# Softmax denominators inverted over 8 columns instead of 512, with the values moved by DMA, in an attention block inside a two-layer encoder trunk

## The chip, the cores and the metric

One Trainium2 chip; the kernel runs on one of its cores. The metric is the device time of one execution in microseconds (us). The engines of a core go by the profile's short names: PE is TensorE (matmuls, and PEld its weight loads), DVE is VectorE, ACT is ScalarE, POOL is GpSimd, SP is SyncE, whose queue issues nearly all DMAs here. Each engine works through its own queue strictly in the order in which the program was written; engines wait for one another by semaphores. SBUF is the on-chip memory of 128 partitions, PSUM the matmul results' memory of eight banks.

## The reference

Two layers, each on x of 512 tokens x 1024 channels in float32:

```python
h = rms_norm(x, attn_norm_g[l])
proj = h @ w_in[l]          # MLA latents, GQA q/k/v, pool channels, 3 branch gates
o_mla  = mla_branch(...)    # 8 heads, q and k of 96 (64 + 32 rotary), v of 64
o_gqa  = gqa_branch(...)    # 8 heads, 2 kv heads, 64 wide, rotary
o_pool = pool_branch(...)   # centred mean pooling
merged = sum(gate_i * (o_i @ w_branch_i))
x = x + merged @ w_out[l]
x = x + (silu(u_gate) * u_val) @ ffn_w_down[l]   # u: conv of width 3 over rms_norm(x) @ ffn_w_up
```

In both attention branches every head is, over all 512 tokens,

```python
p = softmax(q @ k.T * scale)     # 512 x 512
o = p @ v                        # 512 x 64
```

What matters here is the softmax's division: o = (exp(s - m) @ v) / (sum of exp(s - m)), one divisor for each head and token.

## The kernel before

**Precision and matmuls.** Every operand of a matmul is split into a rounded part and a remainder (names ending in h and l, such as wh and wl, ph and pl, oh and ol). A product is three matmuls of the parts. ACT makes the rounded part by a copy, and DVE or POOL makes the remainder by a subtraction. Weights stream in: SP loads pieces of 512 KB into three buffers (raw), ACT makes wh, DVE or POOL makes wl.

**Order.** No scheduler reorders anything: the order on every engine is the order in which the Python code emits instructions. That order is decided by a small planner, class Clock. It keeps an estimated time, an event heap, and for every engine the time at which it would be free. A chain of steps (`chain`) runs one step after the other: each step emits its instructions when the planner's time reaches the end of the step before it. `ck.fin` is that end; a step can set it by hand. `pick` and `copy` choose the engine for a subtraction or a copy by which one the planner holds to be free first (POOL or DVE, and ACT or DVE).

**Attention.** `attention(kind, fill, okey, odst)` runs once for GQA and once for MLA in each layer. Heads 0 to 7 overlap: a table `plan` places each head's steps in time, and between them `fill` emits matmuls of another kind (the gates, the branch projection of the branch finished last, and during GQA the making of MLA's q, k and v with their norms). So PE always has filler work in its queue between the dependent steps of attention. For one head:

- `t_q` (and `t_k` for MLA): transposes q (and k) to channels x tokens, tiles qa, qb, kh, kl;
- `s_max`: scores of 128 queries x 512 keys into the one PSUM bank ps_S, and on DVE their negated row maximum, nm (L224), four times;
- `m_row`: a small matmul turns the four maxima into rows, and DVE writes them into qb (GQA) or qa (MLA), from where a matmul subtracts them;
- `probs`: scores with keys on the partitions, four times 128 keys x 512 queries, into ps_ST; ACT takes the exponential (pe), then ph and pl are made;
- `av_hi`, `av_lo`: values x probabilities into ps_AV. The stationary operand holds a head's 64 value columns and 64 columns of ones, so partitions 0 to 63 of ps_AV are the output and partitions 64 to 127 all hold the same row of 512 sums;
- `o_out(h)`: two heads share the tiles oraw and osum (an even head in partitions 0 to 63, an odd one in 64 to 127). ACT copies the 64 rows of sums and the 64 rows of output out of PSUM. After the odd head DVE inverts osum, 128 x 512, in four reciprocals of 128 columns (L236), multiplies oraw by it, and oh (ACT) and ol (POOL; DVE for the last pair) are made for the branch projection.

The reciprocal works on all 128 partitions, of which 64 and 64 hold the same row. Four pairs a call, four calls: 16 pairs, 64 reciprocals. The branch projection that reads oh and ol of GQA is filler of the MLA attention, and that of MLA comes after the MLA attention.

Of the kernel before, what the change touches and what calls it, by code (L numbers as in the profile page):

```python
# [10 lines left out]
F32 = mybir.dt.float32  # L11
F32R = mybir.dt.float32r
I32 = mybir.dt.int32
AF = mybir.ActivationFunctionType
ALU = mybir.AluOpType
# [3 lines left out]
P = 128  # L19
T = 512  # L20
# [97 lines left out]
class Clock:  # L118
# [37 lines left out]
    def done(self, *key):  # L156
        self.ready[key] = self.fin + self.SEM
# [10 lines left out]
    def chain(self, *steps, after=0.2):  # L168

        def go(n, source=None):  # L170
            if n == len(steps):
                return
            keys, fn = steps[n] if isinstance(steps[n], tuple) else ((), steps[n])
            late = [self.ready.get(k, self.now + 0.5) for k in keys]
            if late and max(late) > self.now:
                self.at(max(late) - self.now, lambda: go(n))
                return
            self.fin, self.source, self.last = self.now, source, None
            fn()
            source, self.source = self.last, None  # L180
            self.at(max(0.0, self.fin - self.now), lambda: go(n + 1, source))
        self.at(after, lambda: go(0))
# [61 lines left out]
def trunk(ctx: ExitStack, tc: tile.TileContext, x, w, prm, gb, cst, out):  # L244
    nc = tc.nc
    ctx.enter_context(tc.manual_schedule())
    ck = Clock()
    at, need, done, chain = ck.at, ck.need, ck.done, ck.chain
    V, A, G = Engine(ck, nc.vector, "DVE"), Engine(ck, nc.scalar, "ACT"), Engine(ck, nc.gpsimd, "Pool")
    PE, SY = nc.tensor, nc.sync  # L250
# [7 lines left out]
    dp = ctx.enter_context(tc.tile_pool(name="dp", bufs=1, space=bass.MemoryType.DRAM))  # L258

    uid = [0]  # L260

    def slot(name, dt=F32):
        uid[0] += 1
        t = sp.tile([P, SLOT], dt, tag="s", name=f"{name}_{uid[0]}")
        return t

    def small(name, shape, dt=F32, bufs=2):
        uid[0] += 1
        t = sm.tile(shape, dt, tag=name, name=f"{name}_{uid[0]}", bufs=bufs)
        return t  # L270
# [12 lines left out]
    def free(tag):  # L283
        heapq.heappush(banks[tag], ck.fin + ck.SEM)
# [86 lines left out]
    def split(hi, lo, src, scale=None, eng=None):  # L371

        steps = []
        if scale is None:
            steps.append(lambda: A.activation(hi, src, AF.Copy))
            steps.append(lambda: (eng or V).tensor_tensor(lo, src, f(hi), ALU.subtract))
        else:
            steps.append(lambda: A.activation(hi, src, AF.Copy, scale=scale))
            steps.append(lambda: V.scalar_tensor_tensor(lo, src, scale, f(hi), ALU.mult, ALU.subtract))
        return steps  # L380
# [108 lines left out]
    def layer(l, sq, xsrc):  # L489
# [510 lines left out]
        def attention(kind, fill, okey, odst):  # L1000
# [156 lines left out]
            def av_lo(h, k):  # L1157
                s = hs[h]
                need(key("pl", h, k))
                vh, vl = vals(h, k)  # L1160
                pl = s.pop(("p", k))[1]
                mm(s["av"], vh, pl[:, :T], False, k == 3)
                if k == 3:
                    o_out(h)

            def o_out(h):
                s = hs.pop(h)
                if h % 2 == 0:
                    ot[:] = [slot("oraw"), slot("osum")]
                raw, sums = ot  # L1170
                js = slice(64 * (h % 2), 64 * (h % 2) + 64)

                def copies():
                    A.activation(sums[js, :T], s["av"][64:128], AF.Copy)
                    A.activation(raw[js, :T], s["av"][0:64], AF.Copy)
                    free("AV")

                def recip(b):
                    bs = slice(b * P, b * P + P)
                    V.reciprocal(sums[:, bs], sums[:, bs])  # L1180

                steps = [copies]
                if h % 2 == 1:
                    oh, ol = slot("oh", F32R), slot("ol", F32R)
                    odst[h // 2] = (oh, ol)
                    steps += [lambda b=b: recip(b) for b in range(4)]
                    steps += [lambda: V.tensor_tensor(raw[:, :T], raw[:, :T], sums[:, :T], ALU.mult),
                              *split(oh[:, :T], ol[:, :T], raw[:, :T], eng=V if h == 7 else G),
                              lambda: done(okey, l, h // 2)]
                chain(*steps)  # L1190
# [67 lines left out]
        for m in range(KC):  # L1258
            tag = tags[m % 3]
# [54 lines left out]
        for c in range(FC):  # L1314
            for part in range(2):
                tag = tags[n % 3]
# [12 lines left out]
        for m in range(KC):  # L1329
            tag = tags[m % 3]  # L1330
# [14 lines left out]
            steps = [resid]  # L1345
# [161 lines left out]
```

## Time and profile before

| | us |
|---|---|
| median of 3 runs | 1699.12 |
| range of the 3 runs | 1698.81 to 1700.99 |
| the profiled execution, its own time | 1701.64 |
| span of the profiled execution | 1699.4 |
| GQA attention, layer 0, from the end of its first pair | 163 to 245 |
| MLA attention, layer 0 | 245 to 373 |
| the same two, layer 1 | 1003 to 1085 and 1085 to 1213 |

The span runs from the first to the last instruction. The profile is one execution, so its stages and durations add up to its own time and not to the median. Busy shares of PE come from modelled ends of matmuls. In the lines of the profile, `out<-in` names tiles without their numbers, xN counts instructions, and "nm L224" means the group of instructions that write nm from line 224. L216, L220, L224, L232 and L236 are the lines of the planner's wrappers for tensor_tensor, scalar_tensor_tensor, tensor_reduce, tensor_copy and reciprocal, so many different steps share a line and are told apart by their tiles. L209 is the same for ACT's activation, L341 for matmuls, L298 for the weight loads on SP.

### The profile page before, as it was taken

The page shows a single profiled execution, that of the slowest core. Times are in us where ns is not written, and L with a number is a line of the kernel's source. Part 1 is how long each engine was busy: PE and PEld are TensorE (multiplying, and loading weights), DVE is VectorE, ACT ScalarE, POOL GpSimd, SP SyncE. Part 2 cuts the span into 40 slices and gives each one's busy share as a digit, 9 for nine tenths or more (in the row PEclk, how much of TensorE's full clock was granted, in tenths as well). Part 3 has the DMA queues.
Part 4 walks back from the last instruction along what each step waited for, and adds up shares of the span by engine and source line. Part 5 has one row for each costly group of instructions (what it writes and reads, how often), then busy time and mean ns, then how long its engine had stood idle before and what let it go on. Part 6 is the DMA issues. An engine that isn't in the chain of part 4 may idle for free.

```text
span 1699.4 us, 20370 instructions
## 1 busy us (share of the span) xinstructions
PE 1655.1 (97%) x7360; PEld 1335.7 (79%) x7360; DVE 938.3 (55%) x1502; ACT 782.6 (46%) x1375; POOL 972.3 (57%) x771
## 2 busy tenths in 40 slices
PE   8889999999999999999999899999999999999999
PEld 7767767778888888888888677777788888888887
DVE  6765976643356666630156759766433666666100
ACT  5356655653344444433234576556534444444221
POOL 4455565764566566655545565666645665666543
PEclk9999999999999999999999999999999999999999
DMA  5221112113423332333333211111233232232331
GB/s 176 85 72 44 56 48 62 38 62 112 124 87 89 98 100 87 100 106 116 100 101 95 70 44 47 61 49 38 75 118 118 87 100 92 94 94 93 111 118 56
DMA packets 44596, 145.40 MB, mean 86 GB/s; under 512 B 5072, under 2 KB 6352, under 8 KB 44496
## 3 DMA queue, kind: packets, MB, share of 16 engines
q1 hardware_dynamic: 44352, 144.10, 27.0%
q8 instruction: 58, 0.95, 0.2%
q14 instruction: 42, 0.34, 0.1%
q10 hardware_dynamic: 144, 0.01, 0.0%
HBM read 139.90 MB, written 4.19 MB: 85 GB/s over the span
## 4 chain that ended last, share of the span: by engine, by line
PE 87%; DVE 8%; issue 2%; ACT 1%; POOL 1%; DMA 0%; SPq 0%; POOLq 0%; DVEq 0%; ACTq 0%
PE ps_acc L341 40%; PE ps_ST L341 23%; PE ps_AV L341 20%; PE ps_S L341 2%; DVE gqr L216 1%; PE ps_mi L345 1%; DVE yt L216 1%; DVE nm L224 1%; POOL wl L216 1%; PE ps_mi L341 1%; DVE MQ L216 1%; DVE yt L220 0%; DVE win L216 0%; DVE y L220 0%; DVE y L228 0%
## 5 line engine op out<-in xcount | busy, mean ns | idle before, releaser
L216 POOL TENSOR_TENSOR wl<-raw,wh 128x512 fp32r<-128x512 f32 (+1 forms) x514 | 678.5, 1330 | 493.4 <-ACT wh L209 432.1
L209 ACT ACTIVATE wh<-raw 128x512 fp32r<-128x512 f32 (+3 forms) x522 | 313.8, 608 | 194.2 <-PE ps_ST L341 70.8
L220 DVE SCALAR_TENSOR_TENSOR a<-u,prm,a 128x512 f32<-128x512 f32 x176 | 239.6, 1362 | 79.2 <-ACT a L209 74.0
L341 PE MATMUL ps_acc<-HH,wh 128*128 128x512 f32 x624 | 247.1, 396 | 2.2 <-DVE XM L220 2.2
L341 PE MATMUL ps_acc<-HH,wl 128*128 128x512 f32 x624 | 246.7, 395 | 1.2 <-POOL wl L216 1.2
L341 PE MATMUL ps_acc<-HL,wh 128*128 128x512 f32 x624 | 246.2, 395 | 0.0
L216 POOL TENSOR_TENSOR pl<-pe,ph 128x512 fp32r<-128x512 f32 x105 | 138.9, 1325 | 110.4 <-ACT ph L209 70.4
L341 PEld LDWEIGHTS ps_acc<-HH,wh 128*128 128x128 f32 x624 | 117.5, 188 | 30.8 <-ACT mns L209 2.1
L341 PEld LDWEIGHTS ps_acc<-HH,wl 128*128 128x128 f32 x624 | 117.3, 188 | 30.0 <-POOL wl L216 2.5
L341 PEld LDWEIGHTS ps_acc<-HL,wh 128*128 128x128 f32 x624 | 117.5, 188 | 26.8
L209 ACT ACTIVATE pe<-ps_ST 128x512 f32<-128x512 f32 x128 | 76.3, 596 | 101.8 <-PE ps_ST L341 100.4
L224 DVE TENSOR_REDUCE nm<-ps_S 128x1 fp32r<-128x512 f32 x128 | 87.8, 686 | 57.3 <-PE ps_S L341 57.0
L216 POOL TENSOR_TENSOR al<-a,ah 128x512 fp32r<-128x512 f32 x44 | 58.1, 1320 | 84.8 <-ACT ah L209 56.5
L341 PE MATMUL ps_AV<-HH,wh 128*128 128x512 f32 x256 | 101.3, 396 | 0.0
L341 PE MATMUL ps_AV<-HH,wl 128*128 128x512 f32 x256 | 101.2, 395 | 0.0
L341 PE MATMUL ps_AV<-HL,wh 128*128 128x512 f32 x256 | 101.1, 395 | 0.0
L341 PE MATMUL ps_ST<-HH,wh 128*128 128x512 f32 x240 | 95.0, 396 | 0.0
L341 PE MATMUL ps_ST<-HH,wl 128*128 128x512 f32 x240 | 94.8, 395 | 0.0
L341 PE MATMUL ps_ST<-HL,wh 128*128 128x512 f32 x240 | 94.8, 395 | 0.0
L209 ACT ACTIVATE a<-u,prm 128x512 f32<-128x512 f32 x88 | 71.8, 816 | 32.4 <-DVE u L216 32.4
L209 ACT ACTIVATE ah<-a 128x512 fp32r<-128x512 f32 x44 | 27.8, 632 | 116.2 <-DVE u L240 110.8
L209 ACT ACTIVATE a<-a 128x512 f32<-128x512 f32 x44 | 27.8, 633 | 113.5 <-DVE u L240 113.5
(332 smaller groups left out, 3563.3 us busy)
## 6 DMA issues: line engine op xcount, KB each, us to landing
raw<-w SPq DMA_DIRECT2D x229, 512.0 KB, 3.5
raw<-w SPq DMA_DIRECT2D x13, 384.0 KB, 3.0
XM<-x SPq DMA_DIRECT2D x16, 256.0 KB, 3.8
raw<-w SPq DMA_DIRECT2D x6, 448.0 KB, 3.4
xsp<-XM SPq DMA_DIRECT2D x8, 256.0 KB, 2.0
XM<-xsp SPq DMA_DIRECT2D x8, 256.0 KB, 3.2
out<-XM SPq DMA_DIRECT2D x8, 256.0 KB, 2.5
raw<-w SPq DMA_DIRECT2D x4, 432.0 KB, 3.2
```

The source lines that it names most:

```text
L209: return self.eng.activation(out, in_, func, **k)
L216: return self.eng.tensor_tensor(out, *a)
L220: return self.eng.scalar_tensor_tensor(out, *a)
L224: return self.eng.tensor_reduce(out, in_, *a, **k)
L341: PE.matmul(o, lhsT=lhsT, rhs=rhs, start=start, stop=stop)
L345: PE.transpose(o, src, ident)
```

## The change

It concerns only `o_out`. For the first three pairs of heads of every call the four reciprocals of 128 columns go. In their place stand a chain of five steps:

1. the copy of the sums takes one row of the 64 equal ones (partition 0 for the even head, 64 for the odd one);
2. `spread`: two DMAs on SP's queue lay each row of 512 sums out as 64 partitions x 8 columns (tile few);
3. `recip`: one reciprocal of 128 partitions x 8 columns on DVE;
4. `write`: one DMA brings the 1024 inverted values to a DRAM tile (line), as two rows of 512;
5. `read`: two DMAs read each row back with a broadcast to 64 partitions (tile oinv), and the multiplication uses oinv.

The planner is told 5, 5 and 6 us for the DMA steps by `ck.fin`, so it places what follows that much later in the order of each engine. The last pair of each call (heads 6 and 7) keeps the copy of 64 rows and the four reciprocals.

```diff
             def o_out(h):
                 s = hs.pop(h)
+                direct = h // 2 == 3
                 if h % 2 == 0:
                     ot[:] = [slot("oraw"), slot("osum")]
                 raw, sums = ot
-                js = slice(64 * (h % 2), 64 * (h % 2) + 64)
+                i = h % 2
+                js = slice(64 * i, 64 * i + 64)
 
                 def copies():
-                    A.activation(sums[js, :T], s["av"][64:128], AF.Copy)
+                    top = 64 * i + (64 if direct else 1)
+                    A.activation(sums[64 * i:top, :T], s["av"][64:64 + top - 64 * i], AF.Copy)
                     A.activation(raw[js, :T], s["av"][0:64], AF.Copy)
                     free("AV")
 
-                def recip(b):
-                    bs = slice(b * P, b * P + P)
-                    V.reciprocal(sums[:, bs], sums[:, bs])
-
                 steps = [copies]
-                if h % 2 == 1:
+                if i == 1:
                     oh, ol = slot("oh", F32R), slot("ol", F32R)
                     odst[h // 2] = (oh, ol)
-                    steps += [lambda b=b: recip(b) for b in range(4)]
-                    steps += [lambda: V.tensor_tensor(raw[:, :T], raw[:, :T], sums[:, :T], ALU.mult),
+                    inv, line = sums, None
+                    if direct:
+                        def recip(b):
+                            bs = slice(b * P, b * P + P)
+                            V.reciprocal(sums[:, bs], sums[:, bs])
+
+                        steps += [lambda b=b: recip(b) for b in range(4)]
+                    else:
+                        few, inv = small("few", [P, 8]), slot("oinv")
+                        uid[0] += 1
+                        line = dp.tile([2, T], F32, tag="line", name=f"line_{uid[0]}", bufs=4)
+
+                        def spread():
+                            for j in range(2):
+                                SY.dma_start(few[64 * j:64 * j + 64], sums[64 * j:64 * j + 1, :T])
+                            ck.fin = ck.now + 5.0
+
+                        def recip():
+                            V.reciprocal(few, few)
+
+                        def write():
+                            SY.dma_start(line.rearrange("j (p f) -> (j p) f", f=8), few)
+                            ck.fin = ck.now + 5.0
+
+                        def read():
+                            for j in range(2):
+                                SY.dma_start(inv[64 * j:64 * j + 64, :T], line[j].partition_broadcast(64))
+                            ck.fin = ck.now + 6.0
+
+                        steps += [spread, recip, write, read]
+                    steps += [lambda: V.tensor_tensor(raw[:, :T], raw[:, :T], inv[:, :T], ALU.mult),
                               *split(oh[:, :T], ol[:, :T], raw[:, :T], eng=V if h == 7 else G),
                               lambda: done(okey, l, h // 2)]
                 chain(*steps)
```

Since the planner now places the steps of these pairs elsewhere and holds DVE to be free earlier, the order of the instructions on all engines differs from the first pair's end on, in both attentions.

## The prediction

> **What bounds the kernel now.** I read the page first, then a table of stages by windows, then TensorE's waits, then VectorE's timeline in the stretch where TensorE waits. On the page:
>
> ```profile
> span 1699.4 us, 20370 instructions
> PE 1655.1 (97%) x7360; PEld 1335.7 (79%) x7360; DVE 938.3 (55%) x1502; ACT 782.6 (46%) x1375; POOL 972.3 (57%) x771
> ```
>
> TensorE (PE) is busy for 97% and the change takes no matmul away, so only the 44 us in which PE stands can be won. The windows of layer 0's attention (columns: length, then busy us of PE, weight load, DVE, ACT, POOL, granted clock, DMA):
>
> ```profile
> 163.00:190.00 27.00, 23.53 (x109) 18.49 (x107) 22.22 (x33) 20.00 (x38) 15.93 (x13) 1.00 0.12 39
> 190.00:245.00 55.00, 50.93 (x227) 38.79 (x226) 49.77 (x83) 35.97 (x64) 32.80 (x27) 0.97 0.14 45
> 245.00:373.00 128.00, 127.86 (x597) 101.78 (x596) 77.38 (x114) 71.85 (x128) 83.49 (x75) 1.00 0.17 53
> 186.60:190.00 3.40, 0.70 (x3) 0.61 (x4) 3.30 (x6) 0.00 (x0) 1.77 (x2) 1.00 0.13 31
> 190.00:193.40 3.40, 3.40 (x10) 2.63 (x9) 3.40 (x7) 1.75 (x3) 0.24 (x1) 0.50 0.30 123
> ```
>
> The GQA attention from its first pair on (first two rows) has 7.5 us of idle PE; the MLA attention (third row) has 0.1 us, so there the change can win nothing. In the last two rows PE stands 2.7 us and is then granted 0.50 of its clock for 3.4 us: matmuls start 0.43 us apart instead of 0.233, which costs 1.6 us more. Layer 1 repeats it (7.3 us idle, 2.55 us of it before 1029.66, then 0.50 until 1033.1). All that could be won is 7.5 + 7.3 + 2 x 1.6 = 18 us. PE's waits between 140 and 260 us say on whom:
>
> ```profile
> PE ps_S L341 <- DVE nm L224: 4.3, 4, 2.7
> PE ps_acc L341 <- DVE XM L220: 1.1, 2, 0.6
> PE ps_acc L341 <- DVE vml L216: 0.9, 1, 0.9
> ```
>
> VectorE (DVE): there is one bank for the scores whose row maximum is taken (ps_S), so each next score matmul waits until DVE's nm has read the last. The longest wait ends with this nm; note what stands ahead of it, and how long:
>
> ```profile
> 184.46 0.19 DVE L216 TENSOR_TENSOR yt<-y,ssm 128x32 f32<-128x32 f32 x1
> 184.68 1.18 DVE L220 SCALAR_TENSOR_TENSOR yt<-yt,y 128x32 f32<-128x32 f32 x1
> 185.90 1.30 DVE L220 SCALAR_TENSOR_TENSOR y<-yt,y 128x32 f32<-128x32 f32 x1
> 187.24 1.18 DVE L216 TENSOR_TENSOR yt<-y,ssm 128x32 f32<-128x32 f32 x1
> 188.46 0.19 DVE L220 SCALAR_TENSOR_TENSOR yt<-yt,y 128x32 f32<-128x32 f32 x1
> 188.56 0.68 DVE L224 TENSOR_REDUCE nm<-ps_S 128x1 fp32r<-128x512 f32 x1
> ```
>
> These are rsqrt steps, not reciprocals. From 181.3 to 232.9 us DVE's timeline has not one row with idle time before it: in this stretch DVE's queue sets PE's pace. Four reciprocals stand in it (pair 1, 202.9 to 210.5); pair 0's stand before it, pair 2's (233.6 to 237.0) behind it, with 2.4 us of DVE idle after them.
>
> **What is removed and added.**
>
> ```profile
> L236 DVE RECIPROCAL osum<-osum x64: 890/941/955, 165.5 to 1216.5; 128x128 f32<-128x128 f32 x64
> L216 DVE TENSOR_TENSOR oraw<-oraw,osum x16: 679/1098/1668, 173.4 to 1220.4; 128x512 f32<-128x512 f32 x16
> ```
>
> Removed: 12 of 16 pairs x 4 = 48 reciprocals x 0.94 = 45 us of DVE. Added on DVE: 12 reciprocals of 8 columns; 7.4 ns a column from this row gives 0.06, and DVE's smallest steps take 0.15 to 0.19, so 0.15 us each, 2 us. The order of the changed program shows what the planner makes of the rest: it gives DVE 22 casts to ph and 2 MK copies that ACT had, and 14 of POOL's pl subtractions: 22 x 0.43 + 2 x 0.69 + 14 x 0.69 = 21 us. Of 45 us, some 22 stay. ACT's sums copy keeps its 512 columns (0.59 us), on 1 partition instead of 64: nothing.
>
> In the MLA attention and everywhere else PE has no idle time, DVE has 40% spare: worth nothing, and it costs nothing as long as that spare time covers the new waits.
>
> **The GQA stretch, per layer.** Per pair the order puts: spread issued after the sums copy; small reciprocal some four DVE steps later; write; read; the multiplication 20 DVE steps on. In DVE's gapless stretch the sum from 181.3 is: four reciprocals away, -3.5; pair 0's multiplication now in it, +1.1; one small reciprocal, +0.15; four more casts, +1.7; an MK copy, +0.7; a reduction that slips in, +0.5. Net +0.6: DVE is no freer here. What does move is the order. The planner puts the row maxima of the last heads ahead of the end of the k norm: yt, yt, ssm, six MK and one XM, which took 6.5 us between 223.0 and 232.9, stand behind the last qb instead of ahead of it. That qb came at 232.9 and comes at 232.9 + 0.6 - 6.5 = 227.0, 5.9 us earlier. PE's matmul that feeds it stands nine 512-wide matmuls (9 x 0.233 = 2.1 us) earlier in PE's own order, which were not saved but put behind. So PE gains 3.8 us. Against that: the first nm after the rsqrt start is now early, but the second stands behind five rsqrt steps and pair 0's multiplication, and head 4's first score waits for its qa, which by the same sum ends at about 204.6, where PE, its matmuls counted in the order at 0.233 us from the first hole on, is there at 202.3. I see two holes of about 2.3 to 2.5 us. They are paid already, since DVE sets the pace, but another half clock (1.6 us) can follow one; at one in two, 0.8 us. Gain: 3.8 - 0.8 = 3.0 us per layer, 6.0 in all. From nothing (the holes cost it all) to 6.5 a layer is possible (7.5 + 1.6 = 9.1, less the waits on vml, mqs and mns that stay, 1.8, and 0.8 of holes); I take 3.0, the sum by the rows.
>
> **The transfers.** Nothing shows transfers this small. The nearest rows (KB, us from issue to landing):
>
> ```profile
> xsp<-XM SPq DMA_DIRECT2D x8, 256.0 KB, 2.0
> XM<-xsp SPq DMA_DIRECT2D x8, 256.0 KB, 3.2
> gb<-gb SPq DMA_DIRECT2D x2, 256.0 KB, 5.1
> prm<-prm SPq DMA_DIRECT2D x1, 89.0 KB, 5.3
> prm<-prm ACTq DMA_DIRECT2D x1, 11.5 KB, 2.9
> ```
>
> Spread and write: 2.0 to 5.3, taken 2.9 (the smallest transfer). Read, 256 KB broadcast in two: 3.2 to 6.4 (the longer gb), taken 4. An issue takes SP 0.33 us. Pair 1: sums copied at 201.5 as now, two issues, spread there at 205.1 (207.5 at worst), small reciprocal not before 206.8; write there at 210.2, read there at 214.9, at worst 220.3; the multiplication's turn is about 217.7. So it is covered by 2.8 us, and missed by 2.6 at worst. The Trainium skill ("DMA: Bandwidth & Descriptors", the anatomy of one DMA) states a fixed cost of about 2.0 us for each; three in turn would land the read at about 212, and the sum would stay; no run here shows it for 32-byte pieces.
>
> On SP the write waits for DVE and the read for the write, with weight loads behind both. raw issued at 183.24 is first read at 204.11 (3.4 us to land), and ACT's list of waits in the attentions has none on raw: some 17 us cover a held queue. ACT's oh and POOL's ol stand in their queues behind each multiplication; the first reader of oh and ol of these pairs comes after the GQA attention (b0, at about 256), of MLA's after the MLA attention.
>
> **Rivals.** (B) The holes eat it: every nm moved forward is paid by a qa or nm moved back. For: +0.6 us of DVE work in the stretch. Against: 6.5 us of steps provably leave its front. Gain 0 to 1.5 a layer: 1697.5, the same.
>
> (C) The landing is late, and this ends slower. Place: pair 1's multiplication in GQA, in DVE's gapless stretch, with head 5's nm behind it and PE behind them. It begins to cost once the chain from small reciprocal to landing passes 10.8 us (206.9 to 217.7), and outweighs the gain by 0.2% once it is about 3 us late (3 + 1.6 of half clock - 3.0 = 1.6 a layer). The rows' highest values make the chain 0.33 + 5.3 + 0.66 + 6.4 = 12.7; if one of the two also queues behind a 512 KB load (3.5 us on the page), 16.2, 5.4 late: 5.4 + 1.6 - 3.0 = 4.0 slower per layer, 1707.1. Against: SP issues a weight load only every 5 to 16 us here.
>
> (D) Exempt work is exchanged for exposed work. Rows: reciprocals keep to 890 to 955 ns, while DVE casts to ph run 398/427/1025 and pl 681/691/1795, long when POOL is in a TENSOR_TENSOR. If each of the 5 casts and copies added to the gapless stretch waits half of POOL's 1.3 us, 3.3 us come back on DVE, the 3.0 are gone, and the time is 1699.7. The median of 427 speaks against so many. The Trainium skill states this as an exclusive lock of a port pair that VectorE and GpSimd share ("SBUF — State Buffer", two separate sides), held by a VectorE instruction with two SBUF inputs or in a two-port mode; by that rule alone the exchange gives (D)'s 1699.7. The 1.18 and 1.30 us rows above, beside POOL's pl from 184.52 to 187.15, agree with it.
>
> That the change does nothing is excluded: the order has 48 fewer reciprocals and 60 new transfers.
>
> **Numbers.** The profiled execution took 1701.64 us (span 1699.4 and 2.2 around it); it lies 2.5 above the median of 1699.12. 1701.64 - 6.0 = 1695.6, which against the median is 1693.1. About 0.2%, 3.4 us, is what a measurement of this kernel tells from no change. Chances: forecast (A) 0.52, faster; (B) 0.18 and (D) 0.10, same; (C) 0.20, slower. The range goes from 1686 (both layers at 6.5) to 1704, which leaves out the upper half of (C) and little else; (A) alone is 1686 to 1695.7.
>
> **What would show it.** Right: PE idle in 163 to 245 falls from 7.5 to about 5 with the k norm's MK steps after the last row maximum; small reciprocals near 0.15 us; DVE total down by some 22 us; no DVE wait on a DMA in attention. (C): "DVE oraw <- DMA oinv" or "DVE few <- DMA few" among DVE's waits, in the GQA stretch. (D): long ph and pl on DVE. A hole over 2.5 us with 0.50 granted behind it in a place that has none now, or any PE idle in 245 to 373, would make the forecast wrong.

## The result, and the profile after

The changed kernel is slower: 1704.99 us, the median of 8 executions (1703.62 to 1707.51), against 1700.31 us for the kernel before on the same chip (8 executions, 1698.81 to 1703.23). The ratio is 1.0027, with a 95% interval of 1.0016 to 1.0038, so 2.7 to 6.5 us. A later comparison gave 1.0026 (1.0016 to 1.0036). The forecast was 1693.1 us.

The profiled execution took 1705.09 us, 3.45 more than that of the kernel before. Its page:

```profile
span 1703.1 us, 20481 instructions
PE 1656.8 (97%) x7360; PEld 1341.4 (79%) x7360; DVE 928.4 (55%) x1504; ACT 768.2 (45%) x1351; POOL 964.5 (57%) x757
```

DVE lost 48 reciprocals, 45 us, and its busy time fell by only 9.9 us. The windows (length, busy us of PE, weight load, DVE, ACT, POOL, granted clock, DMA):

```profile
163.00:190.00 27.00, 24.45 (x114) 19.98 (x113) 19.10 (x36) 19.15 (x37) 16.46 (x14) 0.98 0.14 45
190.00:245.00 55.00, 50.20 (x218) 38.04 (x217) 47.72 (x79) 30.57 (x55) 32.72 (x25) 0.95 0.18 55
245.00:373.00 128.00, 126.88 (x589) 100.21 (x589) 77.41 (x116) 69.67 (x123) 76.48 (x68) 1.00 0.19 60
220.60:224.00 3.40, 0.68 (x2) 0.50 (x2) 3.37 (x6) 0.08 (x1) 2.06 (x2) 0.89 0.00 0
224.00:227.40 3.40, 3.40 (x11) 2.52 (x10) 3.19 (x11) 0.00 (x0) 0.00 (x0) 0.61 0.00 0
```

In GQA (first two rows) PE idles 7.35 us, as long as before (7.5), but the granted clock is lower: 27 x 0.02 + 55 x 0.05 = 3.3 us of clock are lost where 55 x 0.03 = 1.65 were, so two stretches at half clock and not one. The last two rows show the second: PE stands 2.7 us ahead of 223.5, at a place where it did not stand long before, and is slow behind it. MLA (third row), which had 0.1 us of idle PE, has 1.1; in layer 1 it had 0.2 and has 2.5. The two long stalls of PE, and the sums of its waits between 140 and 260 us:

```profile
189.34 0.80 PE L341 MATMUL ps_S<-ka,qa 128*128 128x512 f32 x1 [2.55 <-DVE nm L224]
223.47 0.79 PE L341 MATMUL ps_S<-ka,qa 128*128 128x512 f32 x1 [2.72 <-DVE nm L224]
...
PE ps_S L341 <- DVE nm L224: 6.1, 4, 2.7
PE ps_acc L341 <- DVE vml L216: 0.9, 1, 0.9
```

The waits on XM are gone, those on the row maximum nm have grown from 4.3 to 6.1. DVE's timeline ahead of the new hole, and POOL's beside it:

```profile
217.06 0.68 DVE L216 TENSOR_TENSOR oraw<-oraw,oinv 128x512 f32<-128x512 f32 x1
217.66 1.40 DVE L216 TENSOR_TENSOR kj<-krt 128x128 f32<-128x128 f32 x1
218.98 2.54 DVE L216 TENSOR_TENSOR rp<-krt,tabm 128x64 f32<-128x64 f32 x2
221.45 1.37 DVE L216 TENSOR_TENSOR krr<-krt,tabm 128x128 f32<-128x128 f32 x1
222.73 0.68 DVE L224 TENSOR_REDUCE nm<-ps_S 128x1 fp32r<-128x512 f32 x1
...
217.11 3.10 POOL L216 TENSOR_TENSOR pl<-pe,ph 128x512 fp32r<-128x512 f32 x2
220.17 1.27 POOL L216 TENSOR_TENSOR ol<-oraw,oh 128x512 fp32r<-128x512 f32 x1
221.40 1.26 POOL L216 TENSOR_TENSOR wl<-raw,wh 128x512 fp32r<-128x512 f32 x1
```

kj, rp and krr are the square and the rotation of the keys' rotary part, for the k norm of MLA. They take 5.07 us from 217.66 to the start of nm, and POOL subtracts without a pause beside them. In the kernel before the same rows take 1.19 us from start to nm:

```profile
215.75 0.79 DVE L216 TENSOR_TENSOR kj<-krt 128x128 f32<-128x128 f32 x1
216.47 0.35 DVE L216 TENSOR_TENSOR rp<-krt,tabm 128x64 f32<-128x64 f32 x2
216.74 0.28 DVE L216 TENSOR_TENSOR krr<-krt,tabm 128x128 f32<-128x128 f32 x1
216.94 0.68 DVE L224 TENSOR_REDUCE nm<-ps_S 128x1 fp32r<-128x512 f32 x1
```

The new transfers in the list of DMAs (KB, median us from issue to landing):

```profile
few<-osum SPq DMA_DIRECT2D x24, 2.0 KB, 2.6
line<-few SPq DMA_DIRECT2D x12, 4.0 KB, 1.5
oinv<-line SPq DMA_DIRECT2D x24, 128.0 KB, 3.1
```

The small reciprocals and the products that use them (ns: shortest, median, longest; first and last start):

```profile
L236 DVE RECIPROCAL few<-few x12: 189/193/203, 171.2 to 1202.1; 128x8 f32<-128x8 f32 x12
L216 DVE TENSOR_TENSOR oraw<-oraw,oinv x12: 673/682/1787, 185.3 to 1213.2; 128x512 f32<-128x512 f32 x12
```

DVE's list of waits has two on the new transfers, both in layer 1 and both for the third pair of a call: in GQA the product waits 1.3 us for oinv, at 1093.35 us, and in MLA the small reciprocal waits 2.2 us for few, at 1202.15. Behind the first PE does not wait: its last stall in that stage ends at 1087.9 us.

```profile
1093.35 0.69 DVE L216 TENSOR_TENSOR oraw<-oraw,oinv 128x512 f32<-128x512 f32 x1 [1.35 <-DMA oinv<-line]
1202.15 0.20 DVE L236 RECIPROCAL few<-few 128x8 f32<-128x8 f32 x1 [2.18 <-DMA few<-osum]
```

To place the loss I measured, in every run's trace, two stages between fixed matmuls: GQA from the first transposition of GQA's second group of queries (gqr) to the first of MLA's queries (MQ), and MLA from there to the first matmul on mgh, the merged branches. Windows at half clock move a GQA stage from one execution to the next (in the changed order 112.0 to 114.7 us in layer 0, 111.3 to 113.3 in layer 1), so differences of 1 or 2 us between two profiles are not read in GQA; MLA of one order repeats within 0.7 us. A stall in the text below is the extra distance from one matmul's start to the next; the idle time that the profile prints is some 0.2 us less (the 2.55 and 2.72 above are stalls of 2.7 and 2.9). All ratios are to the kernel before on the same chip. Runs are named by their first letters.

| kernel | GQA, layers 0 and 1 | MLA, layers 0 and 1 | ratio to before, 95% interval |
|---|---|---|---|
| before | 113.1, 112.3 | 185.4, 185.2 | 1 |
| changed | 113.7, 113.0 | 187.1, 187.4 | 1.0027 (1.0016 to 1.0038) |
| e9: changed, again | 113.9, 113.1 | 187.0, 187.6 | 1.0026 (1.0016 to 1.0036) |
| e1: before, no reciprocals | 113.0, 113.8 | 185.2, 185.2 | 0.9996 (0.9985 to 1.0007) |
| e2: changed, no transfers | 112.0, 113.3 | 186.9, 187.1 | 1.0010 (1.0000 to 1.0020) |
| e13: before, with dead transfers | 114.2, 113.5 | 185.3, 185.1 | 0.9992 (0.9982 to 1.0001) |
| e3: changed, rotary steps early | 110.1, 109.6 | 186.9, 187.4 | 1.0005 (0.9995 to 1.0015) |
| e4: before, rotary steps early | 112.5, 112.3 | 185.4, 185.4 | 1.0030 (1.0016 to 1.0043) |
| e6: changed, rotary steps in the idle place | 110.5, 109.8 | 187.0, 187.5 | 0.9986 (0.9977 to 0.9995) |
| e14: before, the same place | 114.3, 115.2 | 185.3, 185.2 | 1.0008 (0.9996 to 1.0020) |
| e16: before, in its widest gap | 113.8, 113.3 | 185.4, 185.3 | 1.0004 (0.9993 to 1.0014) |
| e15: changed, POOL's pl of GQA without inputs | 108.3, 108.1 | 187.0, 187.5 | 0.9963 (0.9948 to 0.9978) |
| e5: changed, MLA's pl back | 114.0, 113.3 | 187.0, 187.5 | 1.0009 (1.0000 to 1.0018) |
| e19: changed, MLA's pl and ph back | 114.7, 113.2 | 186.4, 186.6 | 0.9999 (0.9991 to 1.0007) |
| e18: changed, POOL's pl of MLA without inputs | 114.7, 113.1 | 187.0, 187.6 | 1.0017 (1.0008 to 1.0025) |
| e8: e6 and e5 together | 110.5, 109.4 | 186.9, 187.1 | 0.9985 (0.9976 to 0.9994) |
| e10: the change in GQA alone | 113.3, 111.3 | 185.1, 185.4 | 0.9996 (0.9987 to 1.0005) |
| e11: the change in MLA alone | 114.6, 113.9 | 186.8, 187.1 | 1.0017 (1.0007 to 1.0027) |
| e12: e10 with the steps in the idle place | 110.6, 109.3 | 185.3, 185.2 | 0.9961 (0.9948 to 0.9975) |
| e17: e12 again | 110.3, 109.7 | 185.3, 185.2 | 0.9952 (0.9937 to 0.9968) |

The four stages are 5.3 us longer in the changed kernel's profile (0.7, 1.7, 0.7, 2.2). The rest of the trace, whose work is the same, is 1.6 us shorter, which is within what it varies by from run to run: the 1258 matmuls from mgh to the next stage, for one, took 291.2 to 292.7 us over all these runs, in no relation to the kernel.

### The profile page after: what moved, and what is told of

Its sections match the earlier page's. It is cut to its first block, busy times and chain, and to the rows that moved or that the text cites. A ratio compares the mean times of both kernels' runs of the same rounds, so it can differ in the third digit from the quotient of the medians.

```text
span 1703.1 us, 20481 instructions
## 1 busy us (share of the span) xinstructions
PE 1656.8 (97%) x7360; PEld 1341.4 (79%) x7360; DVE 928.4 (55%) x1504; ACT 768.2 (45%) x1351; POOL 964.5 (57%) x757
## 4 chain that ended last, share of the span: by engine, by line
PE 85%; DVE 8%; issue 3%; ACT 2%; POOL 1%; DMA 1%; SPq 0%; POOLq 0%; DVEq 0%; ACTq 0%
PE ps_acc L341 40%; PE ps_ST L341 22%; PE ps_AV L341 19%; PE ps_S L341 2%; DVE gqr L216 1%; PE ps_mi L345 1%; POOL wl L216 1%; DVE nm L224 1%; DVE MQ L216 1%; PE ps_mi L341 1%; DVE pl L216 1%; DVE rp L216 0%; DVE win L216 0%; DVE yt L216 0%; ACT pe L209 0%
## 5 line engine op out<-in xcount | busy, mean ns | idle before, releaser
L216 POOL TENSOR_TENSOR pl<-pe,ph 128x512 fp32r<-128x512 f32 x91 | 126.3, 1390 | 101.7 <-ACT ph L209 59.4
L209 ACT ACTIVATE a<-a 128x512 f32<-128x512 f32 x44 | 27.8, 632 | 114.2 <-DVE u L240 114.2
```

Of the source, the lines that this page charges most:

```text
L209: return self.eng.activation(out, in_, func, **k)
L216: return self.eng.tensor_tensor(out, *a)
```

## The experiments

**Is it VectorE's time, or the transfers? (e1, e2, e13)** e1 takes the reciprocals out of the kernel before, but still charges the planner for them, so that all else keeps its order:

```diff
                 def recip(b):
                     bs = slice(b * P, b * P + P)
-                    V.reciprocal(sums[:, bs], sums[:, bs])
+                    V._count(sums[:, bs], 0.0084, 0.07)
```

> The kernel before, with all 64 of its reciprocals of 128x128 left out and nothing else changed: every other instruction stands in the same order on the same engine, and the products take the plain sums, so the output is not divided rightly. It frees about 60 us of VectorE (64 x 0.94 us) and adds no transfer. Theory 1 (VectorE's time in the GQA stretch is what TensorE waits for, and the order alone decides what comes of it): the small stalls of GQA go, the first hole of 2.5 us stays; 4 to 6 us a layer less, 1688 to 1692 in all. Rival (what TensorE waits for in GQA is a chain of latencies, VectorE's time is worth little): within 2 us of the kernel before, 1698 to 1700.

Measured: 1701.71 against 1701.83 us, ratio 0.9996. The rival holds. PE's waits between 140 and 262 us are those of the kernel before, to a tenth, and what changes is DVE's, which had no row with idle time between 181.3 and 232.9 (first two rows PE, then DVE between 183 and 237 us):

```profile
PE ps_S L341 <- DVE nm L224: 4.3, 3, 2.8
PE ps_acc L341 <- DVE XM L220: 1.1, 2, 0.6
...
DVE XM L220 <- PE ps_acc L341: 1.9, 1, 1.9
DVE qa L216 <- ACT qa L209: 0.8, 1, 0.8
```

DVE now waits for PE and ACT where it had been inverting. The reciprocals stood in the shadow of those waits; taking away all 60 us of them is worth nothing that can be measured.

e2 keeps the changed order and takes the transfers out (each pair's product reads the plain sums, copied over 64 rows):

```diff
-                            for j in range(2):
-                                SY.dma_start(few[64 * j:64 * j + 64], sums[64 * j:64 * j + 1, :T])
                             ck.fin = ck.now + 5.0
 ...
-                            V.reciprocal(few, few)
+                            V._count(sums[:, :8], 0.0084, 0.07)
```

> The changed kernel without its transfers: its order of all other instructions stays, instruction by instruction, but the 60 transfers and the 12 reciprocals of 128x8 are left out, the sums are copied over 64 rows as in the kernel before, and the products take the plain sums (the output is not divided rightly). Theory 1 (the loss sits in the order on VectorE and GpSimd that the planner made from the freed time): still slower than the kernel before by 3 to 5.5 us, 1703 to 1706, with the hole of 2.7 us at 223.5 us in it. Rival (the loss is the transfers': their landings, the waits for them, what they do to others): back to the kernel before or under it, 1695 to 1700.

Measured: 1703.12 us, ratio 1.0010. The time itself is just inside the theory's window, but over the kernel before it is 1.7 us by the ratio (0 to 3.4) and not 3 or more, 2.7 us less than the changed kernel's. The stages are clearer: MLA is as long as with transfers in layer 0 and 0.3 us shorter in layer 1, where the wait on few is gone, and the holes of 2.6 to 2.9 us in GQA are there. MLA's loss is, but for that 0.3 us, the order's.

e13 does the opposite: the kernel before, with all transfers and small reciprocals beside its own reciprocals and product.

```diff
+                    def mult():
+                        V.tensor_tensor(raw[:, :T], raw[:, :T], sums[:, :T], ALU.mult)
+                        if h // 2 < 3:
+                            chain(spread, lambda: nc.vector.reciprocal(few, few), write, read)
```

> The price of the transfers by themselves: the kernel before in its own order, with its reciprocals and products, and beside them, for the twelve pairs, the 60 transfers and the 12 reciprocals of 128x8 of the changed kernel, whose results nobody reads. Theory (transfers and small reciprocals are hidden): within 1.5 us of the kernel before. Rival (SyncE's waits hold weights back, or the transfers disturb others): 2.5 us or more over it.

Measured: 1701.43 against 1702.55 us, ratio 0.9992. In that order the transfers cost nothing that the time shows; their landings were 2.1, 1.4 and 3.6 us. Nobody waits for them here, so this prices their disturbance and not their latency. One effect is to be seen in the trace: a stall of 1.0 us in the kernel before is 2.1 us long in both layers (at 223.2 and 1063.0). In layer 0 the small reciprocal, 0.19 us, stands ahead of the rsqrt steps and puts them 0.1 us later against POOL's subtractions; two of them now run beside these, 1.31 and 1.29 us long, where one did, 1.18 us.

**The new hole in GQA. (e3, e4, e6, e14, e16)** e3 moves five DVE instructions a layer and charges the planner at the old place, so nothing else moves:

```diff
+        def early():
+            n = nc.vector
+            n.tensor_tensor(kj_, krt, krt, ALU.mult)
+            ...
+            n.tensor_tensor(krr, krr, t2, ALU.add)
+
+        at(17.0, early)
```

> The changed kernel, with five VectorE instructions of a layer moved and nothing else: the square and the rotation of the keys' rotary part (kj, rp twice, krr twice) stand some 20 us earlier in GQA attention instead of behind pair 1's product, just ahead of a score maximum. Theory 1 (the new hole of 2.7 us at 223.5 us is these steps, grown from 1.7 to 5.1 us, and it costs a window of the half clock, 1.6 us, too): 3 to 4.3 us a layer less, 1696 to 1699. Rival 1 (something else is late at the same place, the steps only stand in its shadow): the hole stays, 1703 to 1706. Rival 2 (the steps cost the same wherever they stand, and what waits changes): a hole of the same size elsewhere, 1703 to 1707.

Measured: 1703.07 us, ratio 1.0005. The hole went, as theory 1 had it: GQA fell by some 3.5 us a layer. But by the ratios the time fell by 3.6 us only, not by 6 to 8, since the early place was not free: a row maximum behind it came late and PE stood 1.1 us in layer 0 and 1.7 in layer 1 at 141.6 and 985.8 us, in front of the measured stage.

> The control: the same five VectorE instructions moved to the same early place in the kernel before. Theory 1 (in the kernel before these steps took 1.7 us with no hole behind them): within 1.5 us of the kernel before, 1699 to 1701.5. Rival (the early place is worth something by itself, whatever the reciprocals do): 3 us or more less, 1697 or under, and the same step of the run on the changed kernel then says little about the change.

Measured: 1707.16 us, ratio 1.0030. Slower, which neither theory had. The same 1.1 and 1.7 us stand in front of GQA, which is no shorter and has a stall of 2.1 us that was 1.0 before, and the mean granted clock is 0.990 where the kernel before has 0.993; that is some three windows more (a window of 3.4 us at half clock takes 0.001 off the mean of 1700 us). So the early place is a loss by itself in the kernel before; which of the three it comes from was not separated.

e6 moves the same five steps behind a qb at 163.5 us, where DVE of the changed kernel waits 2.1 us (`at(42.0, early)`).

> The changed kernel with the five steps on the keys' rotary part moved as in the run with the early place, but later: behind the qb at 163.5 us, where VectorE of the changed kernel then waits 2.1 us for an exponential (their 1.7 us fit in it). Theory 1 (these steps cost the hole at 223.5 us and its half clock, and the early place only failed to pay for the 1.1 and 1.7 us that it added there): GQA falls from 113.7 and 113.0 to 109.5 to 110.5 us, with nothing added in front; 6 to 7 us under the changed kernel, 3 to 5 us under the kernel before. Rival (a hole filled is a hole elsewhere: the next score maximum, or another window at half clock): GQA at 111.5 us or more, the time within 2.5 us of the changed kernel's.

Measured: 1700.99 us, ratio 0.9986, with the changed kernel at 1.0026 beside it. GQA is at 110.5 and 109.8, nothing is added in front: 5.6 us won by moving five instructions.

The controls put these steps into the kernel before, behind the same qb (e14, `at(42.0, early)`) and into its widest DVE gap (e16, `at(32.0, early)`).

> The control for the fastest run: in the kernel before, the five steps on the keys' rotary part moved behind the qb at 164.06 us, the same neighbour as in the kernels with the idle place; here the reciprocals of pair 0 stand behind it. Theory A (the gain of the idle place is the change's: the freed time is what the steps need there, and in the kernel before they stood in nobody's way): within 2 us of the kernel before, GQA at 111.5 us or more. Theory B (the gain is the moved steps' alone, and the reciprocals do not matter there either): GQA at 110.5 us or less, 4 to 7 us under the kernel before, equal to the GQA-only run with moved steps.

> A second control, with the steps of the kernel before moved into its widest idle stretch of VectorE, behind the qb at 153.53 us, where it waits 2.13 us for a score; no reciprocal is near. Theory A: within 2 us of the kernel before, GQA at 111.5 us or more. Theory B: as in the run beside it, 4 to 7 us under the kernel before, GQA at 110.5 us or less.

Measured: 1704.93 and 1704.68 against 1702.95 us, ratios 1.0008 and 1.0004; GQA 113.3 to 115.2. Theory A holds. There the steps had been no hindrance, and with them gone the k norm's own steps come earlier, one of them beside POOL: MK takes 1.76 us where 0.68 is usual, and PE stands 2.1 us for the nm behind it.

**Why the steps take four times as long. (e15)** POOL writes zeros in place of its subtraction, in the same order:

```diff
-                    pick(P_BIAS).tensor_tensor(pl[:, :T], pe[:, :T], f(ph[:, :T]), ALU.subtract)
+                    e = pick(P_BIAS)
+                    if gqa and e is G:
+                        e._two(pl[:, :T])
+                        nc.gpsimd.memset(f(pl[:, :T]), 0.0)
+                    else:
+                        e.tensor_tensor(pl[:, :T], pe[:, :T], f(ph[:, :T]), ALU.subtract)
```

> The changed kernel, in which GpSimd's low halves of GQA attention (pl, 52 or so of 64) are written as zeros instead of by a subtraction with two inputs; they keep their place in GpSimd's order, and the output lacks their small share. Theory (a VectorE step with two inputs is stretched while GpSimd reads two inputs): kj and rp at 217.7 to 221 us shrink from 3.9 us to 1.2 or less, though krr beside the wl stays at 1.3; the hole at 223.5 falls from 2.7 us to under 1, GQA to 110 to 112 us, 3 to 6 us under the changed kernel. Rival (the steps are slow there for another reason, such as the waits between them): kj and rp stay at 3 us or more, the hole at 2 or more.

Measured: 1697.24 against 1702.95 us, ratio 0.9963; GQA 108.3 and 108.1, below what the theory gave. DVE at the place of the hole:

```profile
216.53 0.28 DVE L216 TENSOR_TENSOR kj<-krt 128x128 f32<-128x128 f32 x1
216.74 0.35 DVE L216 TENSOR_TENSOR rp<-krt,tabm 128x64 f32<-128x64 f32 x2
217.01 0.28 DVE L216 TENSOR_TENSOR krr<-krt,tabm 128x128 f32<-128x128 f32 x1
217.21 0.68 DVE L224 TENSOR_REDUCE nm<-ps_S 128x1 fp32r<-128x512 f32 x1
```

The same steps in the same order take 0.68 us instead of 5.07, and no hole follows. POOL beside them:

```profile
215.54 0.98 POOL L1136 MEMSET pl<- 128x512 f32 x2
218.08 1.30 POOL L216 TENSOR_TENSOR ol<-oraw,oh 128x512 fp32r<-128x512 f32 x1 [1.56 <-ACT oh L209]
```

The steps had been held up by GpSimd's subtractions. Since zeros are also made faster, 0.5 us instead of 1.3, GpSimd was done at 216.52 and idle while the five steps ran; so this shows what its work beside them cost, and some of the 108 is that POOL is earlier.

**MLA. (e5, e19, e18)** The planner gave DVE six more pl a layer in MLA. The first new stall of PE there, and DVE and POOL ahead of it:

```profile
300.30 0.50 PE L341 MATMUL ps_S<-kh,qa 96*128 96x512 f32 x1 [0.52 <-DVE nm L224]
...
298.06 1.58 DVE L216 TENSOR_TENSOR pl<-pe,ph 128x512 fp32r<-128x512 f32 x1 [0.33 <-ACT ph L209]
299.57 0.68 DVE L224 TENSOR_REDUCE nm<-ps_S 128x1 fp32r<-128x512 f32 x1
...
297.82 1.28 POOL L216 TENSOR_TENSOR XM<-XM,gt 128x512 f32<-128x512 f32 x1 [1.03 <-DVE gt L220]
```

e5 emits these pl on the engines of the kernel before:

```diff
+                        e._two(pl[:, :T])
+                        e = V if (h, k) in PL_DVE else G
+                        e.eng.tensor_tensor(pl[:, :T], pe[:, :T], f(ph[:, :T]), ALU.subtract)
```

> The changed kernel, in which only the engine of MLA's low halves (pl) is set back: per layer the same six of 32 stand on VectorE as in the kernel before, the other 26 on GpSimd, where the changed kernel has twelve on VectorE. Every instruction keeps its place in the order. Theory 1 (MLA's stalls of 0.5 to 0.7 us at 300, 341, 1143 and 1184 us are scores' maxima behind a pl of 1.6 to 1.8 us on VectorE): these stalls go, MLA falls from 187.1 and 187.4 us to 185.2 to 185.8, and the kernel is 3 to 4 us under the changed one. Rival (MLA is longer for another part of the new order, or GpSimd's queue then delays the weights): MLA stays at 186.8 or more, and the time within 1.5 us of the changed kernel's.

Measured: 1704.26 us, ratio 1.0009. The two stalls are gone and MLA is as long as it was. New ones of 0.75 and 0.4 us stand at 317.7 and 342.4: there the product oraw and a cast to ph run 1.49 and 1.52 us beside POOL ahead of an nm, and a pl on POOL is late. The time is nearer to the rival's; that it fell by 2.4 us against e9 goes with the clock (0.9925 against 0.9910 on the mean, 2.5 us), not with the stage.

> The changed kernel with MLA's low halves and casts (pl and ph) all on the engines that the kernel before gives them: per layer six pl and four casts of VectorE fewer, every step in the changed order. Theory (the loss is where steps with two inputs stand, the product's new place among them): one stall goes and another stays, MLA at 186.0 to 187.0. Rival (it is only the number of such steps given to VectorE): MLA at 185.6 or less, 3 to 4 us under the changed kernel.

Measured: 1702.05 us, ratio 0.9999; MLA 186.4 and 186.6. The theory's stage holds, one stall of 0.4 us stays, and two fifths of the 4.0 us that MLA had lost in e9 are gone. The time fell by 4.6 us; 1.6 of it are this stage, and the mean clock of 0.993 against 0.991 in e9 is worth 3.4. Why the clock is higher is not shown: the edit is in MLA, and no profile has a window at half clock there.

> The changed kernel, in which GpSimd's low halves of MLA attention (pl, 40 of the 64 of both layers) are written as zeros and not by a subtraction with two inputs; VectorE's order is untouched, and the output lacks their small share. Theory (MLA's loss, too, is VectorE's steps stretched beside GpSimd just ahead of a score maximum): the oraw product before 317 us takes 0.7 and not 1.8, the stalls at 300, 341, 1143 and 1184 us fall to 0.2 or less, MLA from 187.1 and 187.5 us to 185.2 to 185.8. Rival (the places are late by the order alone): MLA at 186.6 or more.

Measured: 1705.85 us, ratio 1.0017; MLA unchanged. By its own words the rival. But the trace shows that the experiment missed its object: at the stalls the pl on DVE still takes 1.65 us, now as before beside POOL's XM and wl, which I had left. At the product's place the hold-up only moved: in the changed kernel the product takes 1.78 beside a wl and the pl ahead of it 0.68, here the pl takes 1.79 beside that wl and the product 0.68. So MLA's stalls remain unseparated: the long steps stand ahead of them, and no run took the neighbours XM and wl away.

**The sums of the parts. (e8, e10, e11, e12, e17, e9)**

> Both edits of the two runs above in one kernel: MLA's pl on the engines of the kernel before, and the keys' rotary steps in the idle place. Theory 1 (these two places are the whole loss, and the rest of the change is worth a little): the sum of both, 9 to 11 us under the changed kernel and 5 to 7 under the kernel before. Rival (the stalls are not independent, or the transfers cost): less than 6 us under the changed kernel, within 2 us of the kernel before.

Measured: 1699.33 against 1702.75 us, ratio 0.9985: faster than both kernels, but not the sum. It adds nothing to e6 that can be told apart.

e10, e11 and e12 change one line:

```diff
-                direct = h // 2 == 3
+                direct = h // 2 == 3 or not gqa
```

> The change in GQA attention alone: its six pairs (three a layer) go by transfers as in the changed kernel, and MLA's pairs keep their direct reciprocals. Theory (by the segments of both traces MLA loses 1.7 and 2.2 us a layer to its new order, GQA 0.7 a layer): MLA back to 185.2 to 185.6 us, GQA at 113 to 114; 3 to 5 us under the changed kernel, within 2 us of the kernel before. Rival (MLA's loss is only passed on from GQA's order): MLA at 186.8 or more, and the time that of the changed kernel.

Measured: 1701.93 against 1702.55 us, ratio 0.9996; MLA back to 185.1 and 185.4.

> The other half: MLA's six pairs go by transfers, GQA's keep their direct reciprocals. Theory: GQA as in the kernel before (112 to 113.2 us, no hole at 223.5), MLA at 186.8 to 187.6; 3 to 5 us over the kernel before. Rival (GQA's hole and its window at half clock are the loss, MLA's is hidden by the next stage): within 1.5 us of the kernel before.

Measured (with `or gqa`): 1704.89 us, ratio 1.0017; MLA 186.8 and 187.1. MLA's part of the change is a loss of 1.2 to 4.6 us by itself, GQA's is no loss by itself.

> The change in GQA alone, with the keys' rotary steps in the idle place as well. Theory: GQA at 109.5 to 110.5 us and MLA at 185.2 to 185.6; 5 to 8 us under the kernel before and the fastest of all. Rival (MLA in this order has other stalls): MLA at 186.5 or more, no faster than the run with only the rotary steps moved, 1 to 3 us under the kernel before.

> The change in GQA alone with the moved steps once more (it had few rounds), beside the controls on the same chip: 5 to 8 us under the kernel before, GQA at 109.5 to 110.5 us, MLA at 185.2 to 185.6.

Measured: 1695.82 us, ratio 0.9961, and again 1695.88 us, ratio 0.9952 (0.9937 to 0.9968): 4.3 to 8.9 and 5.4 to 10.7 us under the kernel before, the fastest version found. Its waits of PE between 140 and 262 us:

```profile
PE ps_S L341 <- DVE nm L224: 3.5, 3, 2.7
PE ps_acc L341 <- DVE vml L216: 0.9, 1, 0.9
PE ps_ST L341 <- DVE qb L216: 0.5, 1, 0.5
```

The first hole, behind the rsqrt steps, is all that is left of size. The three rows sum to 4.9 us; the same list of the kernel before sums to 7.5 (nm 4.3 and 0.3, XM 1.1, vml 0.9, mns 0.6, mqs 0.3), so some 2.6 us of short waits are gone in this layer.

> The changed kernel itself once more, on the same chip as the runs beside it, so that its edits are compared with it directly and its number of windows at half clock with theirs. If the first comparison holds: 3 to 6 us over the kernel before, granted clock lower by 0.001 to 0.002 on the mean (one or two windows of 3.4 us at half clock more).

Measured: 1706.64 us against 1702.75, ratio 1.0026, mean granted clock 0.9910 against 0.9927.

## Why the prediction was wrong, point by point

Two terms of the sum failed. GQA was to gain 3.0 us a layer and gained nothing that can be told from its spread; MLA was put at nothing and lost 1.7 and 2.2 us, which is most of what was measured.

**"In this stretch DVE's queue sets PE's pace": this premise failed, and with it the 3.8 us.** A timeline without idle time shows that an engine always has something to do, not that it is late. e1 took four reciprocals out of that stretch and PE's stalls stayed the same to 0.1 us. PE's waits end with row maxima (at 188.56 and 222.44 us, for two), and ahead of those no reciprocal stood.

**"That qb comes at 227.0": it came at 230.78.** The order I read was right (the k norm's end stands behind the last qb), the durations were not: I took them from where the steps stood before. kj, rp and krr, 1.4 us there, took 5.3 us in their new place behind pair 1's product, beside four subtractions of POOL, and of the 5.9 us forecast 2.1 remained. This is the term that took GQA's gain away: with these steps elsewhere (e6) the stage is 2.5 us shorter than before in each layer; with them there it is 0.7 longer in the two profiles, which is less than its spread (profiles with the order of the kernel before in GQA have 112.3 to 114.6, those with the changed order 111.3 to 114.7). That e6's 2.5 lies near the forecast 3.0 does not save the premise: what is gone in that order is some 2.6 us of short waits (e12's list), not a qb 5.9 us earlier.

**"Two holes of 2.3 to 2.5 us, another half clock at one in two."** Two holes came, 2.55 and 2.72 us, one where forecast and the other for another reason (an nm behind the rotary steps, not a qa). Both were followed by half clock in both layers, so one more window came, 1.6 us of clock and not 0.8. In the stage it cost less: with the same order and holes and no window, e2 took 112.0 in layer 0 and e10 111.3 in layer 1, against 113.7 and 113.0 with two, so two windows were worth some 1.7 us. PE, slower behind a hole, waits less at what comes next: e2's layer 0 has waits of 0.5 us on qb and 0.4 on qa that the changed kernel has not.

**"MLA: worth nothing, and it costs nothing": the second half failed.** It cost 1.7 and 2.2 us, without transfers too (e2), and the change in MLA alone is slower (e11). I looked only at DVE's spare time there (40%) and not at which instructions would stand ahead of each nm. Six more pl a layer and the moved product do; with pl and casts put back two fifths of the loss went (e19), and the rest is not separated.

**Rival (D) named the mechanism and was given 0.10.** It priced it at half of POOL's 1.3 us for five casts and copies, held against it the casts' median of 427 ns, and ended at "the same". Casts were not the steps concerned: their median stayed at 428, and 22 more of them added 9.2 us to DVE, near the 9.5 forecast. The subtractions pl were: 14 more added 15.7 us and not 9.7. Small steps were, too, which I had seen in the very first hole (1.18, 1.30, 1.18 us in place of 0.19) and not carried to the other small steps that the new order moves. In the traces of both kernels, the 37 steps of 32 columns on yt and y that overlap no subtraction of POOL take 0.18 to 0.19 us; of the 26 that one overlaps for over 30% of their time, 18 take 0.5 to 1.3 us and 8 stay at 0.2. Reciprocals take 0.938 and 0.941 us, and nm 0.690 and 0.691, alone and beside POOL. The Trainium skill ("SBUF — State Buffer", who interferes with whom) says that a VectorE instruction with two SBUF inputs contends with GpSimd's reads, while one with at most one input outside the two-port modes does not. The runs agree: reciprocals and nm have one input and were not held up, and in e15 and e18 the eleven steps with two inputs that ran beside the writing of zeros, and beside no subtraction, took their usual time (0.67 to 0.69 us at 512 columns, 0.19 at 32).

**The transfers were priced about right, and covered.** 2.6, 1.5 and 3.1 us against 2.9, 2.9 and 4, and e13 shows no cost. The write's 1.5 us is less than the fixed cost of about 2.0 us that the prediction took from the Trainium skill ("DMA: Bandwidth & Descriptors", the anatomy of one DMA), in a section on transfers issued by GpSimd; the measurement decides. Rival (C), on which I had put the whole chance of "slower", showed its sign once in GQA, for the third pair of layer 1, where PE did not wait behind it, and once in MLA; pair 1, its place, was covered.

**Clock.** The mean granted clock was 0.9927 over 147 executions of the kernel before and 0.9913 over 19 of the changed one. 0.0015 of 1700 us is 2.5 us, one to two windows at half clock. It must not be added to MLA's loss as it stands. No profile has a window at half clock in an MLA stage, and these stages alone are 3.9 us longer, most of the 4.4 to 4.7 us; e11 (MLA alone, 1.2 to 4.6 us slower) and e10 (GQA alone, 2.2 us faster to 0.9 slower) agree. In GQA the second hole and its half clock stand against short waits that went, and the sum is about nothing. How the windows of single executions fall was not studied.

**What stays open:** the larger part of MLA's loss by cause (above), and whether a part of the changed kernel's loss needs the transfers: by the ratios e2 lost 2.7 us less than the changed kernel, with an interval of 1.7 us to either side for e2 alone, while its stages differ by 0.3 us in MLA.

## What to carry to other kernels

Freed time on an engine that never idles is worth nothing unless what the critical engine waits for lies behind it: leave the work out, keep the order, and see (e1), before building anything to replace it. When a planner reorders, cost each step anew by its neighbours in the new place: steps of VectorE with two SBUF inputs just ahead of a critical reduction and beside GpSimd's subtractions are what to look for, and moving five of them into an idle place was worth 5.6 us in the changed order, and nothing in the kernel before (e14), where they held nobody up. Work that GpSimd does not hold up, here the reciprocals, is good filler; exchanging it for work that it does hold up can lose.

## What the runs showed of the hardware beyond what I had expected

Beside GpSimd's subtractions of 1.3 us, a step of VectorE grew by up to some 1.1 us whatever its size: from 0.19 us to 1.3 at 32 columns, from 0.21 (e16) to 1.27 at 64, from 0.68 to 1.8 at 512. So small steps suffer most. Holes of 2.55 and 2.72 us were followed by 3.4 us at half clock in both layers of the changed kernel, and in e13 so were holes in which PE was idle for 1.9 us; but it is not certain, since holes as long in layer 0 of e2 and layer 1 of e10 had no half clock behind them in the stage. And three transfers in a row through DRAM, of 2, 4 and 128 KB, took 2.6, 1.5 and 3.1 us to land and cost nothing that the time could show (e13).
